# PSUM banks by name, key loads in pairs, softmax sums inverted for four blocks at once, first output products inside the attention

## The chip, the core and the metric

The kernel runs on one core of one Trainium2 chip. Its engines each work through an instruction list in order: TensorE (PE, and PEld for its weight loads) multiplies matrices into PSUM, VectorE (DVE) does element-wise work and reductions, ScalarE (ACT) copies and exponentials, GpSimd (POOL) further element-wise work, and SyncE (SP) issues the DMA transfers. The metric is the time of one execution on the device in microseconds (us).

## The reference

One layer of a block with two branches: top-k sparse attention (a) and multi-scale pooling (b), joined by gates. Sequence 4096, model width 1024, 8 heads of 64 on 2 groups of keys, 128 queries to a block. Cut to what matters:

```
proj = rms_norm(x, norm_g) @ w_in             # q k v, index qi ki wi, z_a, u_b, z_b, gates
# attention, for each block of 128 queries:
iscore = sum_h relu(qi_h . ki) * wi_h          # over allowed (chunk-causal) keys
_, idx = lax.top_k(iscore, 256)
a = (softmax(q . k[idx] / 8) @ v[idx]) * silu(z_a)
b = multiscale_pool(u_b, pool_w, pool_scale) * silu(z_b)
y = sigmoid(g_a) * (a @ w_branch_a) + sigmoid(g_b) * (b @ w_branch_b)
out = x + y @ w_out
```

## The kernel before

All products run in three float32r passes over a high and a low part (high x high, high x low, low x high). The "split" of a tile makes these parts: ScalarE copies the high part, VectorE subtracts it (lines 235 and 237 for weights, 1440 and 1441 for activations).

The program has five stages. `phase1` (to 442 us) normalizes x, projects q, k, v and the index parts, and stores rows in DRAM (`hlD`, `rowD`, `hD`). `phase_index` (442 to 2086) computes the index scores and their top-k threshold, and between them the dense products of gates and pooling (lines 1043 to 1045). `phase_exact` (to 2099) is a branch that is skipped here. `phase_attention` (2099 to 3564) runs 64 units (b, g): query block b = 0 to 31, key group g = 0 and 1, each with b + 1 tiles of 128 keys. `phase_out` (3564 to 4316) runs 16 column blocks c of 256 tokens: 16 products of 12 matmuls (8 row blocks m of y, for branch a and branch b, lines 1475 to 1477, tile `pa`), the gates (1503, 1508), and the output product (tile `po`).

From `phase_index` on a `Plan` sets the order. Steps are added with an engine, a cost and a key; `Plan.run` plays them through with these costs and writes each engine's instructions in the resulting order, the smallest key first among those that can start. A ring of buffers (`pl.ring`, `pl.new`) holds a step back until a buffer is free; `pl.have` puts a tile in a given place of a ring. On the chip each engine then keeps that order, and waits where a semaphore isn't set yet.

In a unit of the attention TensorE computes logits a first time for the row maxima (tile `ps`, line 1267), which VectorE reduces (1273) and combines (`mf`, 1279). SP stores the maxima and reads them back into `qm` (1281, 1282). TensorE then computes the transposed logits (`st`, 1306 and 1307), VectorE adds the bias (1310), ScalarE takes the exponential (1313), TensorE multiplies with v (`pv`, 1322) and sums over keys (1358, with GpSimd's running sums `acc`, 1337). ScalarE copies the sums (`sm`, 1362); SP stores them (1369) and reads them back, spread over partitions (`rl`, 1371); VectorE inverts them (1372) and SP stores the inverses (`invD`, 1373). `phase_out` reads `invD` (tile `r`, 1461) and multiplies. Loads of keys (`k4`) and of v are issued block by block, and TensorE turns the keys (335). Near the end of the attention the weights of the branches are loaded through the ring `raw` in pieces of 256 columns (229) and split (`wb`, then `wa`).

At the border of `phase1` and `phase_index` the first dense product takes a PSUM bank that the last projection (tile `ma`, read by line 417) had used. The last block's index key `k31` is loaded from `hlD` and turned on TensorE with key -50 (line 706). `guess` starts with a small product (line 629) on a tile that lines 601 and 602 write.

## Time and profile before

| | us |
|---|---|
| median of three runs | 4315.23 |
| lowest and highest | 4313.32 and 4319.19 |
| the profiled execution | 4317.85 |
| its span, first to last instruction | 4316.1 |
| TensorE busy in the span | 4154.3 (96%) |
| VectorE busy | 3223.0 (75%) |
| mean granted clock of TensorE | 0.982 |

The span is what the profile divides up; 1.75 us of the profiled execution lie around it. A wait is read as "instruction <- what ended its wait: total, times, longest". In an operation's name the tile that is written stands ahead of the arrow. A granted clock of 1.00 is 2.4 GHz, and 0.5 is 1.2 GHz; a window's number is the mean over it.

### The profile page before, as it was taken

How to read it: one execution, taken by the hardware profiler on the slowest of the kernel's cores; microseconds unless marked ns; L12 is line 12 of the kernel's file. 1: busy time of each engine (PE TensorE's matmuls, PEld its weight loads, DVE VectorE, ACT ScalarE, POOL GpSimd, SP SyncE). 2: the span in 40 equal slices, each digit the busy share in tenths (PEclk: the TensorE clock that was granted, in tenths of full speed). 3: DMA queues.
4: the chain of work that ended last, by engine and by line, in shares of the span. 5: the costliest groups of instructions: out<-in, count | busy, mean ns of one | idle time of the engine just before them, and what ended most of it. 6: DMA issues, size and time to landing. Idle time of an engine off the chain costs nothing. (4 is left out here: it accounts for less than half of the span.)

```text
span 4316.1 us, 77051 instructions
## 1 busy us (share of the span) xinstructions
PE 4154.3 (96%) x27746; PEld 3497.2 (81%) x27747; DVE 3223.0 (75%) x7858; ACT 2347.8 (54%) x3993; POOL 1904.1 (44%) x1717
## 2 busy tenths in 40 slices
PE   8999899999999999999789999999999997999999
PEld 7989899999998999999556666666666656999998
DVE  5555688888889788787568889999999994434342
ACT  5444687777777877887355555555555552111110
POOL 3454222323224332010057788888999981111110
PEclk9999999999999999999799999999999998999999
DMA  6666544545444446666532212222211116444442
GB/s 224 246 242 235 191 163 168 181 175 184 160 172 163 162 167 213 208 230 212 145 65 63 59 44 45 49 49 52 45 37 38 24 31 198 149 133 152 137 142 81
DMA packets 461117, 586.36 MB, mean 136 GB/s; under 512 B 165886, under 2 KB 358970, under 8 KB 456507
## 3 DMA queue, kind: packets, MB, share of 16 engines
q1 hardware_dynamic: 460730, 581.40, 41.9%
q8 instruction: 219, 3.59, 0.4%
q14 instruction: 168, 1.37, 0.1%
HBM read 388.54 MB, written 175.54 MB: 131 GB/s over the span
## 5 line engine op out<-in xcount | busy, mean ns | idle before, releaser
L1043 PE MATMUL pd<-h,wgh 128*128 128x256 f32 x3584 | 1019.6, 284 | 9.6 <-ACT row L417 8.2
L1044 PE MATMUL pd<-h,wgh 128*128 128x256 f32 x3584 | 1012.7, 283 | 0.0
L1045 PE MATMUL pd<-h,wgl 128*128 128x256 f32 x3584 | 1012.0, 282 | 0.0
L1337 POOL TENSOR_TENSOR acc<-acc,tt 128x1024 f32<-128x1024 f32 x388 | 925.5, 2385 | 114.0 <-ACT tt L1313 92.5
L1313 ACT ACTIVATE tt<-tt 128x512 f32<-128x512 f32 x1056 | 652.7, 631 | 583.2 <-DVE tt L1310 580.4
L1310 DVE TENSOR_TENSOR tt<-st,bT 128x512 f32<-128x512 f32 x1056 | 694.0, 685 | 65.8 <-PE st L1307 60.0
L1043 PEld LDWEIGHTS pd<-h,wgh 128*128 128x128 f32 x3584 | 681.2, 190 | 28.1 <-ACT row L417 8.5
L761 DVE SCALAR_TENSOR_TENSOR ring<-rl,wi,ring 128x1024 f32<-128x1024 f32 (+7 forms) x624 | 690.6, 1149 | 11.3 <-ACT rl L759 8.5
L1044 PEld LDWEIGHTS pd<-h,wgh 128*128 128x128 f32 x3584 | 682.0, 190 | 14.7
L1273 DVE CUSTOM_DVE_ANT_0 jk<-ps,bias 128x1024 bf16<-128x1024 f32 (+7 forms) x640 | 656.1, 1029 | 34.5 <-PE ps L1267 33.6
L1045 PEld LDWEIGHTS pd<-h,wgl 128*128 128x128 f32 x3584 | 681.9, 190 | 0.0
L759 ACT ACTIVATE rl<-ps 128x1024 f32<-128x1024 f32 (+7 forms) x624 | 539.4, 890 | 133.3 <-PE ps L756 61.4
L1322 PE MATMUL pv<-tt,vv 128*64 128x256 f32 x4224 | 527.9, 391 | 0.0
L846 ACT ACTIVATE sg<-ring,tk 128x2048 fp8e4<-128x2048 f32 (+7 forms) x322 | 485.4, 1509 | 37.3 <-DVE tk L833 21.2
L1306 PE MATMUL st<-qa,kk 128*128 128x512 f32 x1056 | 456.2, 432 | 15.9 <-DVE tt L1310 14.6
L1322 PEld LDWEIGHTS pv<-tt,vv 128*64 128x64 f32 x4224 | 280.8, 138 | 212.1 <-issue 76.8
L1307 PE MATMUL st<-qm,kl 65*128 65x512 f32 x1056 | 422.0, 400 | 3.2 <-DMA qm<-maxD 3.2
L1508 POOL TENSOR_TENSOR ga<-ga,gb 128x256 f32<-128x256 f32 x128 | 102.8, 810 | 638.8 <-DVE gb L1503 386.6
L1267 PE MATMUL ps<-kk,qa 128*128 128x512 f32 (+3 forms) x1152 | 363.0, 392 | 17.8 <-DVE mx L1273 17.7
L756 PE MATMUL ps<-kis,qT 128*128 128x512 f32 (+3 forms) x1136 | 335.1, 382 | 13.3 <-ACT rl L759 13.2
L1440 ACT ACTIVATE yh<-ga 128x256 fp32r<-128x256 f32 x128 | 53.5, 418 | 521.1 <-PE po L1476 314.4
L1306 PEld LDWEIGHTS st<-qa,kk 128*128 128x128 f32 x1056 | 200.4, 190 | 162.3 <-DVE tt L1310 59.3
(322 smaller groups left out, 7816.3 us busy)
## 6 DMA issues: line engine op xcount, KB each, us to landing
h<-hD SPq DMA_DIRECT2D x192, 1024.0 KB
hlD<-rhl SPq DMA_DIRECT2D x32, 1280.0 KB
gD<-sgm SPq DMA_DIRECT2D x256, 128.0 KB
x<-x SPq DMA_DIRECT2D x32, 512.0 KB
wraw<-w_in SPq DMA_DIRECT2D x32, 512.0 KB
hD<-hh SPq DMA_DIRECT2D x32, 512.0 KB
hD<-hl SPq DMA_DIRECT2D x32, 512.0 KB
q<-hlD SPq DMA_DIRECT2D x32, 512.0 KB
```

What stands on the lines that cost most here:

```text
L759: r = pl.add("act", 0.05 + n * 0.834e-3, k_, lambda ps=ps, rl=rl, n=n: act.activation(rl.t[:, :n], ps.t[:, :n], AF.Relu), [m], use=[ps, rl])
L761: prev[o] = pl.add("dve", 0.1 + n * 1.04e-3, k_, lambda rl=rl, o=o, n=n, h=h: v.scalar_tensor_tensor(acc[:, o:o + n], rl.t[:, :n], self.wi ...
L846: mine.append(pl.add("act", 0.28 + m * 0.834e-3, key, lambda sg=sg, o=o, m=m, e=e, j=j, b=b: act.activation(sg.t[:, o:o + m], where[b][:, ...
L1043: pe.matmul(out, wh.t[:, k], r1, start=(k == 0), stop=False)
L1044: pe.matmul(out, wh.t[:, k], r2, start=False, stop=False)
L1045: pe.matmul(out, wl.t[:, k], r1, start=False, stop=(k == KT - 1))
L1273: v.tensor_tensor_reduce(out=jk.t[:, :n], in0=ps.t[:, :n], in1=BI[b][0].t[:, o:o + n], scale=1.0, scalar=-3e38, op0=OP.add, op1=OP.max, ac ...
L1306: pe.matmul(s.t, kk[:, g, o], qa.t[:, hs], start=True, stop=False)
L1310: ad = pl.add("dve", 0.602, i, lambda s=s, tt=tt, r=r, kt=kt: v.tensor_tensor(tt.t[:, r], s.t, bc(bt.t[:, kt:kt + 1], [P, 4, P]), op=OP.ad ...
L1313: E[kt] = pl.add("act", 0.52, i, lambda tt=tt, r=r: act.activation(tt.t[:, r], tt.t[:, r], AF.Exp), [ad], use=[tt])
L1322: pe.matmul(pv.t[64 * f:64 * f + 64], vv[:, k, 64 * g:64 * g + 64], T[k // 2].t[:, k % 2, 2 * f:2 * f + 2], start=(k == 0), stop=(k == b))
L1337: gp.tensor_tensor(acc.t, first, tt.t, op=OP.add)
```

## The change

- **Index border.** Six `pl.have` lines fix which PSUM banks come first in `phase_index`. The turn of `k31` gets key 12 in place of -50.
- **Keys.** `k4` and v are loaded for two blocks by one DMA each; the ring has two buffers of twice the size.
- **Sums.** A unit only stores its sums. After the eighth unit of four blocks, `inverse` adds one load of 128x32, one reciprocal and one store, with keys 12 and 18 after the unit's end. The last four blocks are inverted in `phase_out` (key 100), and r loads of those blocks wait for it.
- **Tail.** Weights are loaded in pieces of 512 columns, ring of two. Split b and the gates of column block 0 are loaded inside the attention, and its first four products of branch b are written there. `wa`'s second half is loaded in `phase_out`; `wo` is waited for by column half. The order of products is b 4, b 5, a 0, a 1, b 6, b 7, a 2 to a 7 in block 0, and b ahead of a elsewhere.

The core of the diff:

```diff
-K4 = 4
+K4 = 2
 DIR = 4
-CL = 2
-WOK = 30.0
+WOK = 45.0
 WOD = 0.0
 PVN = 4
+IVL = 12.0
...
-            cs = slice(c, c + self.w)
-
-            def load(raw=raw, cs=cs):
+            cs = slice(o, o + w)
+
+            def load(raw=raw, o=c * CH + o):
                 for p0, r0, n, src in rows:
-                    self.queue.dma_start(raw.t[p0:p0 + n], src[r0:r0 + n, cs])
+                    self.queue.dma_start(raw.t[p0:p0 + n], src[r0:r0 + n, o:o + w])
             s = pl.add("dma", 1.4, key - 20, load, after, use=[raw])
...
+
+        for name, i in (("ps", 0), ("pd", 0), ("pd", 1), ("pd", 2), ("pt", 0), ("ps", 1)):
+            pl.have(name, i)
...
-        s3 = pl.add("pe", 0.06, -50, lambda: self.turn(pk.t[:, 0], k31), [sk], use=[pk])
+        s3 = pl.add("pe", 0.06, 12, lambda: self.turn(pk.t[:, 0], k31), [sk], use=[pk])
...
         def keys(b, base):
 
-            rows = slice(b * P, (b + 1) * P)
-            k4, pt = new("k4"), new("st")
+            k4 = new("k4")
 
             def load():
-                sp_dma(k4.t.rearrange("p g c -> p (g c)").bitcast(F32), self.hlD[rows, H_K:H_QI])
-                sp_dma(vv[:, b], self.rowD[rows, R_V - R_QI:])
+                two = slice(b * P, (b + 2) * P)
+                sp_dma(k4.t.rearrange("p t g c -> p t (g c)").bitcast(F32),
+                       self.hlD[two, H_K:H_QI].rearrange("(t p) c -> p t c", p=P))
+                sp_dma(vv[:, b:b + 2], self.rowD[two, R_V - R_QI:].rearrange("(t p) c -> p t c", p=P))
...
             s3 = pl.add("dma", 0.2, end + FD, store_sums, [s2], use=[sm])
-            s4 = pl.add("dma", 0.2, end + FD, lambda: sp_dma(rl.t, flat(self.sumD)), [s3], [rl])
-            s5 = pl.add("dve", 0.12, end + FD + FE, lambda: v.reciprocal(rl.t, rl.t), [s4], use=[rl])
-            pl.add("dma", 0.2, end + FD + FE, lambda: sp_dma(flat(self.invD), rl.t), [s5], use=[rl])
+            summed.setdefault(b // 4, []).append(s3)
+            if len(summed[b // 4]) == 8 and u < len(units) - 1:
+                self.inverse(pl, b // 4, end + IVL, summed[b // 4])
...
-                first += 1
+                first += 2
...
-        pl.ring("raw", 3, lambda i: self.wp.tile([P, CH // 2], F32, name=f"raw{i}"))
-        src = a["w_branch_a"][0]
-        self.wa, self.wb = (Weights(self, pl, n, 4, nc.sync, CH // 2) for n in ("wa", "wb"))
+        w2 = 2 * P
+        pl.ring("raw", 2, lambda i: self.wp.tile([P, CH], F32, name=f"raw{i}"))
+        for name, bufs, dt in (("o", 1, F32), ("bh", 2, F32R), ("bl", 2, F32R), ("gb", 2, F32)):
+            pl.ring(name, bufs, lambda i, name=name, dt=dt: self.wp.tile([P, 2, w2], dt, name=f"{name}{i}"))
+        self.wa, self.wb = (Weights(self, n, 4, nc.sync) for n in ("wa", "wb"))
...
+        for c in range(2):
+            for k in range(4):
+                self.wb.put(pl, c, k, E0 - 40 + c * 10, [(0, k * P, P, a["w_branch_b"][0])], lambda: self.wp, CH, [s])
...
+                s1 = pl.add("pe", 1.32, E0 + PRE + m, mm, [x[2] for x in xs] + self.wb.steps[0], use=[ps])
...
         for k in range(4):
-            self.wb.put(k, at[-1] - 40, [(0, k * P, P, a["w_branch_b"][0])], lambda: self.wp, [s])
-        for k in range(4):
-            self.wa.put(k, at[-1] - 20, [(0, k * 64, 64, src), (64, 256 + k * 64, 64, src)], lambda: self.wp, [s])
+            self.wa.put(pl, 0, k, E0 - 15, self.rows_a[k], lambda: self.wp, CH, [s])
...
+    def inverse(self, pl, n, key, after):
+
+        nc = self.nc
+        rl = pl.new("rl")
+
+        def flat(d):
+            return bass.AP(tensor=d.tensor, offset=d[4 * n].offset, ap=[[32, P], [1, 32]])
+        s = pl.add("dma", 0.2, key, lambda: nc.sync.dma_start(rl.t, flat(self.sumD)), after, [rl])
+        s = pl.add("dve", 0.12, key + 6, lambda: nc.vector.reciprocal(rl.t, rl.t), [s], use=[rl])
+        return pl.add("dma", 0.2, key + 6, lambda: nc.sync.dma_start(flat(self.invD), rl.t), [s], use=[rl])
...
+        pl.ring("rl", 1, lambda i: sp.tile([P, 32], F32, name=f"rl{i}"))
+        inv = self.inverse(pl, NB // 4 - 1, 100.0, [])
+        pl.ring("raw", 4, lambda i: (self.wp if i < 2 else sp).tile([P, CH], F32, name=f"raw{i}"))
...
-                s2 = pl.add("dma", 1.0, key - 15, spread, use=[r])
+                s2 = pl.add("dma", 1.0, key - 15, spread, [inv] if 2 * c >= NB - 4 else [], use=[r])
...
-        for k in range(KT):
-            wo.put(k, WOK + k * WOD, [(0, k * P, P, a["w_out"][0])], lambda: sp)
+        for k in range(4):
+            self.wa.put(pl, 1, k, 12.0, self.rows_a[k], lambda: sp, CH)
+        for c in range(2):
+            for k in range(KT):
+                wo.put(pl, c, k, WOK + 4 * c, [(0, k * P, P, a["w_out"][0])], lambda: sp, CH)
...
-            lag = CL if c == 0 else 0
-            for m, b in sorted(((m, b) for m in range(8) for b in "ba"), key=lambda x: (x[0] + lag * (x[1] == "a"), x)):
+            if c == 0:
+                out = {(m, "b"): (first["gb"][m // 2], None) for m in range(4)}
+            order = sorted(((m, b) for m in range(8) for b in "ba"), key=lambda x: x[0] + (x[1] == "a") * (2 if c == 1 else 0.5))
+            if c == 0:
+                order = [(4, "b"), (5, "b"), (0, "a"), (1, "a"), (6, "b"), (7, "b")] + [(m, "a") for m in range(2, 8)]
+            for m, b in order:
...
-                             lambda k, i, fs=fs: wo.parts[i][:, k, fs], wo.steps + [y[2] for y in Y], key,
+                             lambda k, i, fs=fs: wo.get(i, k, fs), wo.steps[f] + [y[2] for y in Y], key,
```

**Index border, TensorE.** Before: the dense product (`pd`) with line 335's turn of the key, then line 629; `qi` are the index queries.

```order
L1045 MATMUL pd_5325<-h_4959,wgl_4972 128x256
L335 MATMUL pt_5344<-identr,k_5260 128x128
L1043 MATMUL pd_5325<-h_4959,wgh_4971 128x256
L1044 MATMUL pd_5325<-h_4961,wgh_4971 128x256
L1045 MATMUL pd_5325<-h_4959,wgl_4972 128x256
L1043 MATMUL pd_5325<-h_4959,wgh_4971 128x256
L1044 MATMUL pd_5325<-h_4961,wgh_4971 128x256
L1045 MATMUL pd_5325<-h_4959,wgl_4972 128x256
L629 MATMUL pd_5353<-ring 128x1
L335 MATMUL pt_5355<-identr,qi_5314 128x128 x4
```

The turn stands inside the second set of dense matmuls.

After, the same place (line numbers are those of the changed file: 1052 to 1054 the dense product, 635 the small product, 341 the turns):

```order
L1052 MATMUL pd_5331<-h_4959,wgh_4971 128x256
L1053 MATMUL pd_5331<-h_4961,wgh_4971 128x256
L1054 MATMUL pd_5331<-h_4959,wgl_4972 128x256
L635 MATMUL pd_5356<-ring 128x1
L341 MATMUL pt_5358<-identr,qi_5320 128x128 x4
L1052 MATMUL pd_5331<-h_4959,wgh_4971 128x256
```

The key's turn is gone from here; it stands later, and six more dense matmuls stand ahead of the small product.

**Early attention, VectorE.** Before, `tt` is the bias addition, `jk` and `mx` the maxima, `rl` the sums to invert:

```order
L1372 RECIPROCAL rl_29208<-rl_29208 128x4
L1273 ISA jk_29238,mx_29171<-ps_29222,bias_28856 128x768
L1273 ISA mx_29171 128x1
L1310 TENSOR_TENSOR tt_29249<-st_29231,bT_28986 128x512
L1310 TENSOR_TENSOR tt_29249<-st_29241,bT_28986 128x512
L1273 ISA jk_29269,mx_29270<-ps_29244,bias_29039 128x896
L1273 ISA mx_29270 128x1
L1279 TENSOR_REDUCE mf_29274<-mx_29171 128x4
L1310 TENSOR_TENSOR tt_29276<-st_29251,bT_28986 128x512
L1273 ISA jk_29282,mx_29270<-ps_29255,bias_29039 128x896
L1273 ISA mx_29270 128x1
L1372 RECIPROCAL rl_29267<-rl_29267 128x4
```

One reciprocal stands there for each unit, between maxima and additions.

After, around the first reciprocal of a group:

```order
L1286 ISA jk_29306,mx_29247<-ps_29292,bias_29025 128x896
L1286 ISA mx_29247 128x1
L1323 TENSOR_TENSOR tt_29299<-st_29301,bT_29121 128x512
L1323 TENSOR_TENSOR tt_29333<-st_29316,bT_29121 128x512
L1286 ISA jk_29337,mx_29338<-ps_29321,bias_29025 128x896
L1286 ISA mx_29338 128x1
L1292 TENSOR_REDUCE mf_29353<-mx_29247 128x4
L1464 RECIPROCAL rl_29244<-rl_29244 128x32
L1323 TENSOR_TENSOR tt_29333<-st_29348,bT_29121 128x512
L1286 ISA jk_29365,mx_29338<-ps_29355,bias_29025 128x896
L1286 ISA mx_29338 128x1
L1323 TENSOR_TENSOR tt_29374<-st_29361,bT_29121 128x512
```

The reciprocal after each unit is gone; one of 128x32 stands there for eight units.

**Output border, SP.** Before, from the last sums on: `raw` are weights on their way, `o`, `z` and `r` the parts of the branches' inputs:

```order
L1371 DMA rl_42525<-sumD 128x4
L229 DMA raw_42527<-w_branch_a 64x256 x2
L229 DMA raw_42532<-w_branch_a 64x256 x2
L229 DMA raw_42538<-w_branch_a 64x256 x2
L1373 DMA invD<-rl_42525 128x4
L1452 DMA o_42559<-bD 128x2x256
L1452 DMA o_42561<-bD 128x2x256
L1455 DMA o_42563<-oD 128x2x256
L1456 DMA z_42565<-gD 128x2x256
L1461 DMA r_42571<-invD 64x2x128 x4
```

The loads of `o`, `z` and `r` stand behind the weights and the last sums' way out and back.

After, from the last weight piece of the attention on:

```order
L234 DMA raw_42129<-w_branch_a 64x512 x2
L1388 DMA oD<-ov_42210 64x2x128 x2
L1379 DMA sumD<-sm_42227 1x256 x2
L1514 DMA z_42286<-gD 128x2x256
L1519 DMA r_42301<-invD 64x2x128 x4
L1513 DMA o_42306<-oD 128x2x256
L1514 DMA z_42308<-gD 128x2x256
L1519 DMA r_42311<-invD 64x2x128 x4
L1562 DMA ga_42319<-gD 128x2x256
L234 DMA raw_42323<-w_branch_a 64x512 x2
```

The last sums' load and their inverses' store no longer stand here, and the loads of branch b stand earlier.

**Output border, TensorE.** After, the end of the attention: `ps_42168` and `ps_42214` are the first two of the four products of branch b:

```order
L1444 MATMUL ps_42168<-bl_41968,wb_41847 128x256
L1444 MATMUL ps_42168<-bh_41953,wb_41848 128x256
L1335 MATMUL pv_41902<-tt_42134,vv 64x256 x4
L1335 MATMUL pv_41902<-tt_42160,vv 64x256 x4
L1371 MATMUL st_42191<-acc_41914,ones 64x256 x2
L1371 MATMUL st_42191<-tt_42090,ones 64x256 x4
L1371 MATMUL st_42191<-tt_42119,ones 64x256 x4
L1371 MATMUL st_42191<-tt_42134,ones 64x256 x4
L1371 MATMUL st_42191<-tt_42160,ones 64x256 x4
L1444 MATMUL ps_42214<-bh_41882,wb_41847 128x256
```

Before, the last `pv` and the sums of line 1358 follow each other, and the first product of branch b stands behind them as `pa`. Now one product stands ahead of the last `pv`, and three follow the sums.

## Rows read from the trace of the kernel before

**Rows 1.** Windows: us; busy us (count) of PE, PEld, DVE, ACT, POOL; clock, DMA.

```profile
2147.00:2530.00 383.00, 353.43 (x2023) 225.99 (x2021) 308.70 (x631) 197.66 (x368) 261.91 (x130) 0.96 0.29 61
2530.00:3500.00 970.00, 969.66 (x5672) 642.36 (x5671) 918.94 (x1706) 524.60 (x913) 869.43 (x387) 1.00 0.18 40
3564.00:3625.00 61.00, 36.27 (x221) 32.92 (x218) 31.62 (x62) 20.05 (x40) 8.13 (x8) 0.76 0.63 187
```

**Rows 2.** Waits of VectorE, 2090 to 2560: total us, times, longest.

```profile
DVE rl L1372 <- DMA rl<-sumD: 51.8, 24, 5.4
```

**Rows 3.** Waits of TensorE, 2147 to 2530.

```profile
PE ps L1267 <- DVE mx L1273: 17.1, 11, 4.5
PE st L1306 <- DVE tt L1310: 8.8, 8, 3.7
```

**Rows 4.** Chain of waits, shares by line: 2147 to 2530, then 2530 to 3500.

```profile
by line: PE pv L1322 18.7%; PE ps L1267 10.2%; PE st L1306 10.1%; PE st L1307 8.1%; DMA rl<-sumD 7.1%; issue 4.7%; DVE tt L1310 4.2%; DVE jk L1273 3.8%; DMA sumD<-sm 3.2%; PE st L1358 1.8%; PE st L335 1.7%; DMA maxD<-mf 1.5%; ACT tt L1313 0
...
by line: PE pv L1322 36.6%; PE st L1306 22.0%; PE ps L1267 19.3%; PE st L1307 18.1%; PE st L1358 1.6%; PE st L335 1.5%; DMA rl<-sumD 0.4%; DMA sumD<-sm 0.1%; SPq L1378 0.1%; DVE tt L1310 0.1%; ACT qa L1232 0.1%; ACT qm L1233 0.0%; issue 0.0
```

**Rows 5.** Groups by line, the bias addition: 2147 to 2530, then 3000 to 3500.

```profile
L1310 DVE TENSOR_TENSOR tt<-st,bT 128x512 f32<-128x512 f32 x245 | 161.9, 684 | 17.9 <-PE st L1307 16.5 <-issue 0.6 <-PE ps L1267 0.2
...
L1310 DVE TENSOR_TENSOR tt<-st,bT 128x512 f32<-128x512 f32 x395 | 259.4, 685 | 16.5 <-PE st L1307 13.9 <-POOL acc L1337 0.6
```

**Rows 6.** Waits of TensorE, 440 to 470.

```profile
PE pd L1043 <- ACT row L417: 8.2, 1, 8.2
PE pt L335 <- DMA k<-hlD: 6.1, 1, 6.1
```

**Rows 7.** Timeline of ScalarE and VectorE, 460 to 465.5: start, us, instruction, wait ahead.

```profile
462.62 0.31 ACT L572 ACTIVATE wm0h<-sgm 128x128 fp32r<-128x128 f32 x1 [5.96 <-DMA sgm<-pool_w]
...
464.57 0.17 DVE L602 MEMSET ring<- 128x128 f32 x1
```

**Rows 8.** Waits of TensorE, 3564 to 3640.

```profile
PE pa L1475 <- ACT bh L1440: 16.6, 1, 16.6
PE po L1475 <- ACT yh L1440: 5.5, 1, 5.5
PE pa L1475 <- ACT ah L1440: 2.0, 1, 2.0
```

**Rows 9.** Timeline of SyncE's DMA issues, 3562 to 3580.

```profile
3566.14 0.67 SPq L1369 DMA_DIRECT2D sumD<-sm  x2
...
3575.05 0.59 SPq L1373 DMA_DIRECT2D invD<-rl  x1
```

**Rows 10.** Pieces of the chain, 3555 to 3625: start, us, what.

```profile
3559.38 2.28 DMA raw<-w_branch_a
...
3570.69 1.77 DMA rl<-sumD
...
3577.18 6.59 DMA z<-gD
...
3585.06 3.33 DMA r<-invD
...
3614.16 3.92 DMA raw<-w_out
```

**Rows 11.** Windows after 3581, columns as in rows 1.

```profile
3581.00:3588.00 7.00, 6.44 (x30) 5.65 (x30) 3.97 (x6) 1.26 (x2) 0.00 (x0) 0.66 0.76 192
...
3597.00:3616.00 19.00, 19.00 (x148) 18.24 (x146) 12.80 (x26) 8.70 (x17) 5.54 (x5) 1.00 0.61 186
```

**Rows 12.** Groups by line from 3516 and 3564, timelines of DVE and POOL from 3524.

```profile
L237 DVE TENSOR_TENSOR wb<-raw,wb 128x256 fp32r<-128x256 f32 x16 | 21.4, 1337 | 0.0
...
L237 DVE TENSOR_TENSOR wo<-raw,wo 128x512 fp32r<-128x512 f32 x16 | 10.8, 688 | 3.3 <-ACT wo L235 3.0
...
3525.57 2.00 DVE L237 TENSOR_TENSOR wb<-raw,wb 128x256 fp32r<-128x256 f32 x1
...
3524.84 15.04 POOL L1337 TENSOR_TENSOR acc<-acc,tt 128x1024 f32<-128x1024 f32 x6
```

More of the change, by code (lines that the diff above doesn't have):

```diff
@@ L51 @@
 QB = 3
-WQ = 0
+PRE = 4
 OV = 2
@@ new lines, in phase_attention @@
+        self.wa, self.wb = (Weights(self, n, 4, nc.sync) for n in ("wa", "wb"))
+        self.rows_a = [[(0, k * 64, 64, a["w_branch_a"][0]), (64, 256 + k * 64, 64, a["w_branch_a"][0])] for k in range(4)]
+        s = pl.add("dma", 0.1, at[-1] - 60, room, done)
+        E0 = at[-1]
+        self.first = {"gb": []}
+        for c in range(2):
+            for k in range(4):
+                self.wb.put(pl, c, k, E0 - 40 + c * 10, [(0, k * P, P, a["w_branch_b"][0])], lambda: self.wp, CH, [s])
+        xs = []
@@ new lines, in phase_attention @@
+        for i in range(2):
+            o, h, l = new("o"), new("bh"), new("bl")
+            s1 = pl.add("dma", 1.0, E0 - 45, lambda o=o, i=i: sp_dma(
+                o.t, self.bD[2 * i:2 * i + 2, :, 0:w2].rearrange("k p c -> p k c")), [s], use=[o])
+            s1 = pl.add("act", 0.52, E0 - 25, lambda o=o, h=h: act.activation(h.t, o.t, AF.Copy), [s1], use=[o, h])
+            s1 = pl.add("dve", 0.61, E0 - 25, lambda o=o, h=h, l=l: v.tensor_tensor(
+                l.t, o.t, h.t.bitcast(F32), op=OP.subtract), [s1], use=[o, h, l])
+            xs.append((h, l, s1))
@@ new lines, in phase_attention, with mm @@
+        for i in range(2):
+            g = new("gb")
+            s0 = pl.add("dma", 1.0, E0 - 45, lambda g=g, i=i: sp_dma(
+                g.t, self.gD[8 + 2 * i:10 + 2 * i, :, 0:w2].rearrange("k p c -> p k c")), [s], use=[g])
+            for m in (2 * i, 2 * i + 1):
+                ps = new("ps")
+                def mm(ps=ps, m=m):
+                    ms = slice(m * P, (m + 1) * P)
+                    for k in range(4):
+                        for x, y in ((0, 0), (0, 1), (1, 0)):
+                            pe.matmul(ps.t[:, :w2], self.wb.get(x, k, ms), xs[k // 2][y].t[:, k % 2],
+                                      start=(k == x == y == 0), stop=(k == 3 and x == 1))
+                s1 = pl.add("pe", 1.32, E0 + PRE + m, mm, [x[2] for x in xs] + self.wb.steps[0], use=[ps])
+                pl.add("dve", 0.34, E0 + PRE + m, lambda g=g, ps=ps, m=m: v.tensor_tensor(
+                    g.t[:, m % 2], ps.t[:, :w2], g.t[:, m % 2], op=OP.mult), [s0, s1], use=[g, ps])
+            self.first["gb"].append(g)
@@ L1429, in phase_out @@
                       "al": (AB, two, F32R), "bh": (AB, two, F32R), "bl": (AB, two, F32R), "ga": (GB, two, F32),
-                      "gb": (GB, two, F32), "yh": (YB, one, F32R), "yl": (YB, one, F32R)}),
+                      "gb": (3, two, F32), "yh": (YB, one, F32R), "yl": (YB, one, F32R)}),
                 (pp, {"pa": (4, [P, CH], F32), "po": (2, [P, CH], F32)})):
             for name, (bufs, shape, dt) in rings.items():
-                pl.ring(name, bufs, lambda i, name=name, pool=pool, shape=shape, dt=dt: pool.tile(
-                    shape, dt, name=f"{name}{i}"))
+                pl.ring(name, bufs, lambda i, name=name, pool=pool, shape=shape, dt=dt: (
+                    self.wp if i < kept.get(name, 0) else pool).tile(shape, dt, name=f"{name}{i}"))
+        first = {n: [pl.have(n, i, x.t) for i, x in enumerate(self.first[n])] for n in ("bh", "bl", "gb")}
         def split(key, name, src, after, n):
@@ L1487, in phase_out @@
             cs = slice(c * w2, (c + 1) * w2)
-            X = {b: [load(c, k, c * T - LDC, b) for k in (0, 2)] for b in "ba"}
+            X = {b: [load(c, k, c * T - LDC, b) if c or b == "a" else (first["bh"][k // 2], first["bl"][k // 2], None)
+                     for k in (0, 2)] for b in "ba"}
             Y, out, G = [], {}, {}
-            lag = CL if c == 0 else 0
-            for m, b in sorted(((m, b) for m in range(8) for b in "ba"), key=lambda x: (x[0] + lag * (x[1] == "a"), x)):
+            if c == 0:
[4 more added lines that the diff above has]
+            for m, b in order:
                 key = c * T + m * T / 8
@@ L1498, in phase_out @@
                 g, s0 = G[b]
-                x, pa, w = X[b], new("pa"), wa if b == "a" else wb
-                s1 = product(4, lambda pa=pa: pa.t[:, :w2], lambda k, i, w=w, ms=ms: w[i][:, k, ms],
-                             lambda k, i, x=x: x[k // 2][i].t[:, k % 2], [y[2] for y in x] + [s1], key,
+                x, pa, w = X[b], new("pa"), self.wa if b == "a" else self.wb
+                s1 = product(4, lambda pa=pa: pa.t[:, :w2], lambda k, i, w=w, ms=ms: w.get(i, k, ms),
+                             lambda k, i, x=x: x[k // 2][i].t[:, k % 2], [y[2] for y in x] + [s1] + (
+                                 self.wa.steps[1][-4:] if c == 0 and b == "a" and m >= 4 else []), key,
                              [pa] + [h for y in x for h in y[:2]], w2)
```

64 lines of the change are left out of this document (35 added, 29 removed).

## The prediction

> **What bounds the kernel now.** I read the busy time of each engine by stage first, then what TensorE and VectorE wait for, then the chain of waits. In the late attention (2530 to 3500 us) TensorE is busy in all but 0.34 of 970 us at full clock, with VectorE at 918.94: nothing there waits, and only work taken off TensorE itself could shorten it [rows 1]. In the early attention (2147 to 2530) it is busy in 353.43 of 383 us, and VectorE, with 308.70, is not full either: the two engines stop in turns. The largest wait of VectorE in the early part is the reciprocal of line 1372, which waits for the load of the sums just stored: 51.8 us in 24 waits [rows 2]. VectorE works in its written order, so the maxima and the bias additions behind that reciprocal stop too, and TensorE then waits for exactly these: 17.1 us for maxima and 8.8 us for additions [rows 3]. The chain of waits in that stretch gives 7.1% to that load and 3.2% to the store ahead of it, that is 27.2 + 12.3 = 39.5 of 383 us; in the late attention the two have 0.4% and 0.1%, 4.9 of 970 us [rows 4].
>
> Two other idle places are borders. At 442 us TensorE waits 8.2 us for a PSUM bank that ScalarE's copy of line 417 still reads, then 6.1 us for a key load [rows 6]. After 3564 us it waits 16.6 us for the first split of branch b, 2.0 for branch a and 5.5 for the first y [rows 8], and works at part of its clock between the waits: 0.66 granted at 3581 to 3588 against 1.00 after 3597 [rows 11]. The stretch 3564 to 3625 holds only 36.27 us of TensorE work in 61 us [rows 1].
>
> **Sums inverted late, for four blocks at once.** This removes 64 loads, reciprocals and stores and adds 8 of each. In the new order VectorE's reciprocal of a group stands about two units of maxima behind the position at which SP issues its load in the first groups, and about one unit or less in the last. The load itself was 1.77 us in the chain at the output border [rows 10]; a unit of the early attention lasts several times that (245 score tiles in 383 us are 1.56 us a tile, and a unit of block b has b + 1 of them) [rows 5]. So I cost the eight new waits at 0, covered by the additions and maxima between. If that cover is gone at all eight places, they cost 8 x 1.77 = 14 us. On SP the loads wait in line for the last of eight stores, as each load did before; behind them stand stores of maxima and loads of queries, which now meet 8 such stops in place of 64.
>
> What of the 51.8 us comes back? Not less, in principle, than TensorE's own idle time behind VectorE, 17.1 + 8.8 = 25.9 us [rows 3], and not more than the 39.5 us of the chain unless the engines fall into step better than now. A check by rate: 395 tiles took 500 us in the late part, 1.27 us each; at that rate 245 tiles are 310 us, 73 less than the stretch took [rows 5]. Early units are short, so what each unit pays once (sums, turns of the queries) weighs more on a tile, and part of the 73 stays. I take 33 us, the middle of 25.9 and 39.5. For the range: down to 15, should VectorE, with 308.70 of 383 us busy, be late next for its own work and half of TensorE's idle time stay; up to 45. The late attention gives 0 to 4.9; I take 3. Next late is what rows 3 name without the reciprocal: TensorE's scores waiting for a free bank behind VectorE's maxima.
>
> **Order of PSUM banks, turn of the last key.** No work is removed. The first bank of the dense product is now one that is free at 442, and the key's turn stands behind 42 dense products in place of 36. TensorE can then do these 42 from 442 on. But the next thing in its order, the product of line 629, needs the memset of line 602 at 464.57, which stands on VectorE behind ScalarE's splits of the pool weights at 462.62, which wait 5.96 us for their load [rows 7]. None of these moves on its queue. TensorE stood at line 629 at about 465 and will stand there again, with its idle time in one piece. I take 0, between -14.3 (both waits gone, 8.2 + 6.1) and +2 (a clock that rises again later).
>
> **Keys in pairs.** 64 load issues become 32, with the same bytes. A turn that waits for its pair waits for the larger load; the first query's load, which ends the wait at the start of the attention, stands behind the same number of issues. I take 0, from -1 to +1.
>
> **First products in the attention's tail.** Removed from the border: the last sums' round trip on SP (load at 3570.69 [rows 10], store at 3575.05, then the first loads of the output stage [rows 9]), 16 narrow weight loads for branch b become 8 wide ones, half of branch a's move behind the border, and 4 of the 16 products of the first column block are done early. One product is 12 matmuls; 148 matmuls took 19.00 us [rows 11], so one is about 1.5 us and four are 6. The walk: TensorE ends the sums at about 3564 as now and goes on at once with three of these products and two more of branch b, to about 3571.5. Branch a needs z and r, whose issues stand behind the store of the last sums (now at 3566.14 [rows 9]). The z load took 6.59 us and the r load 3.33 [rows 10]; with the weights of a no longer ahead, I put the last of them at 3574 to 3576 and the first product of a at 3574 to 3577: 2 to 6 us idle. The next product of b needs a PSUM buffer freed by VectorE behind the splits of branch a's second half: 3 to 5 us idle. The first output product needs the halved w_out loads, the last of which landed in 3.92 us [rows 10]: 0 to 5 us idle, and 1.5 for the first y. Together 6.5 to 17.5 us idle where 16.6 + 2.0 + 5.5 = 24.1 were [rows 8]. The stretches at half clock cost now: 0.66 over 7 us and the like twice more, about 8 us; with two or three gaps again I keep 5 to 8. With one product (1.5 us) already done before the sums, the gain is 24.1 - 17.5 + 0 + 1.5 = 8 to 24.1 - 6.5 + 3 + 1.5 = 22. I take 12, nearer the lower end, since each gap above is one of SP's order, which is issued at about 0.6 us an entry.
>
> Rows 11 show that TensorE came back from 16.6 us of idleness at a clock of 0.66 and was at 1.00 from 3597 on. The Trainium skill, "TensorE: Matmul & The Clock Gate", section "What's actually happening", states that idle TensorE drops to 1.2 GHz and only sustained work lifts it to 2.4. The trace agrees. By this rule several short gaps could keep the five early b products at the lower level: 5 x 1.5 = 7.5 us lost, and the border would gain 4 or 5 in place of 12. I leave it at the bottom of the term's range, 2.
>
> In the attention's tail itself 16 splits of 256 columns become 14 of 512 (8 of wb, 2 of b, 4 of wa). Alone a split of 512 takes 688 ns. Beside GpSimd's running sums the 16 took 1337 ns each, 21.4 us in all; the one of 2.00 us began at 3525.57 and ended at 3527.57, just after GpSimd's second 2.51 us step from 3524.84 began (six in 15.04 us) [rows 12]. So a split waits for GpSimd's instruction to end and then runs: the wait is per instruction, not per column. 14 x (1.34 + 0.3) = 23 us, against 21.4: within 2 us, taken as 0.
>
> **Sum.** 33 + 3 + 0 + 0 + 12 = 48 us. The profiled execution took 4317.85 us, so its like would take 4269.9; the median of the three runs, 4315.23, is 2.6 lower, and I forecast 4315.23 - 48 = 4267 us.
>
> **Rivals.**
> First, the reciprocal's waits only hid what VectorE and TensorE need anyway. For it: VectorE is at 81% in the stretch, 94.7% in the late part [rows 1]. The early term is 15, the late one 0, and the time 4315 - 15 - 12 = 4288. Against it: the chain gives the load 7.1%.
> Second, all of the 51.8 us comes back: 4315 - 52 - 5 - 12 = 4246. Against it: TensorE has only 29.6 us of idle time in that stretch.
> Third, the index border gives its 14.3 us as well: 4253. It needs line 602 to be early, and rows 7 speak against that. That the new order there gains nothing is what I forecast.
> Fourth, the split beside GpSimd loses time by columns, not by instructions: 14 x 2.67 = 37 in place of 21.4 us, and VectorE is full in that stretch, so 16 us on the end: 4283. The Trainium skill, "GPSIMD Engine Reference", section "Specifications", says that GpSimd shares its SBUF interfaces with VectorE and contends with instructions of two SBUF inputs; a contention shared element by element would give this time. The ends in rows 12 speak for whole instructions.
> Fifth, slower: the wide weight loads of the tail have a ring of two and their splits stand between the bias additions on VectorE and the exponentials on ScalarE. Were no load to overlap another's split, a round would be two issues (1.2), landing (2.28 to 3.92 [rows 10]), ScalarE's half (0.6), VectorE's (0.7 to 2): up to 7.7 us, and 12 rounds 92 us where the stretch of rows 12 has 41 now: +51, which with the attention's 36 us and the border's 12 gone makes 4315 - 36 + 51 = 4330. It turns slower than before from 12 rounds of 6.4 us on (77 against 41 + 36), that is if landing takes nearly its longest at every round. Two to five additions stand between a split and the next but one, and landing was 2.28 us, so the overlap should hold.
>
> **Chances.** Forecast 0.52, first rival 0.20, second 0.10, third 0.06, fourth 0.07, fifth 0.05. The range must leave out no more than 2 in 10: from 4238 (second rival with 20 at the output border) to 4298 (first rival with 2 there). About 0.2%, 8.6 us, is what a measurement of this kernel can tell from no change: faster than 4306.6 has 0.90, within 0.06, slower 0.04.
>
> **What would show it.** Right: in the early attention no wait of VectorE for the load of sums worth naming, TensorE's busy share there above 0.97, and the late attention as before within 5 us. At 442 us one wait of TensorE for line 602 or its product up to 465. At the output border TensorE's waits of 10 to 17 us in three pieces. Wrong: a new wait of the 128x32 reciprocal, a wait of ScalarE's or VectorE's splits for weights inside the attention's tail, or the early stretch still long with VectorE full.

## The result and the profile after

| | before | after |
|---|---|---|
| median of four runs, us | 4314.4 | 4263.1 |
| lowest and highest | 4313.32, 4319.19 | 4260.26, 4264.02 |
| ratio, 95% interval | | 0.9878 [0.9861, 0.9895] |
| profiled execution, us | 4317.85 | 4264.02 |
| its span, us | 4316.1 | 4262.3 |
| TensorE busy, us | 4154.3 | 4137.7 |

The kernel became 51 us faster; 48 were forecast, and the median of 4267 that was forecast lies 4 us above the one measured. To see where the time went I compare where the same matmuls start in the two traces, so that each stretch holds the same work. A score tile is one tile `st` of 128 keys for a unit; the 192nd matmul of the output product (`po`) is the last of the second column block.

| stretch, by starts of matmuls | before, us | after, us | gained | forecast |
|---|---|---|---|---|
| start to the first transposed logits of the attention (`st`) | 2123.7 | 2127.2 | -3.5 | 0 |
| to the 300th score tile (early attention) | 466.6 | 426.8 | 39.8 | 33 |
| to the 1000th (late attention) | 894.9 | 896.0 | -1.1 | 3 |
| to the last sum of the attention (its tail) | 78.7 | 81.6 | -2.9 | 0 |
| to the 192nd matmul of the output product (border) | 142.8 | 121.3 | 21.5 | 12 |
| to the last matmul | 605.3 | 605.2 | 0.1 | 0 |

The windows of the early attention, from the first score tile to the 300th, in the columns of [rows 1]: the stretch, busy us (and counts) of PE, PEld, DVE, ACT and POOL, then the clock. Of before:

```profile
2123.70:2590.30 466.60, 432.77 (x2441) 276.30 (x2440) 377.15 (x785) 240.15 (x445) 312.63 (x154) 0.95 0.29 61
```

and of after:

```profile
2127.20:2554.00 426.80, 417.81 (x2437) 273.11 (x2437) 375.52 (x755) 238.84 (x445) 313.26 (x154) 0.97 0.30 66
```

TensorE was idle for 33.8 us of it and is now for 9.0. That is 24.8 us. The other 15.0 us are busy time, 432.77 against 417.81, for the same work, at a mean clock of 0.95 against 0.97. The windows of the stretch in which the granted clock was 0.50, added up, six of before and four of after (their length, then the busy time of each engine):

```profile
sum 44.90, PE 38.25 PEld 22.05 DVE 27.70 ACT 15.86 POOL 13.68; mean PE 6.37 PEld 3.68 DVE 4.62 ACT 2.64 POOL 2.28
...
sum 21.20, PE 18.31 PEld 10.47 DVE 7.05 ACT 8.36 POOL 2.53; mean PE 4.58 PEld 2.62 DVE 1.76 ACT 2.09 POOL 0.63
```

So 20 us less of TensorE's work ran at the lower clock. At the output border of the changed kernel matmuls of one product start 0.12 us apart at 1.00 and 0.21 at 0.50; by that, an estimate, the clock makes about 9 of the 15.0 us. The other 6 weren't traced. VectorE's waits, 2090 to 2560, are now

```profile
DVE tt L1323 <- PE st L1320: 23.2, 36, 3.0
DVE jk L1286 <- PE ps L1280: 20.0, 31, 3.8
DVE jk L1286 <- POOL bT L1256: 8.4, 1, 8.4
```

with no wait for the load of the sums among them (51.8 us in [rows 2]); the engine waits for TensorE instead, which is now the bound. In the chain of waits of 2147 to 2530 the load of the sums is no longer among the large shares (7.1% in [rows 4]); the store ahead of it still has 1.2% (3.2% before):

```profile
by line: PE pv L1335 34.4%; PE st L1319 20.4%; PE ps L1280 18.6%; PE st L1320 16.4%; PE st L1371 3.8%; PE st L341 3.1%; DMA sumD<-sm 1.2%; SPq L1259 0.7%; SPq L1388 0.3%; DVE jk L1286 0.3%; issue 0.2%; ACT sm L1375 0.2%; SPq L1379 0.2%; SPq
```

The eight reciprocals of groups take twice the 0.17 us that one of a unit took (count, then shortest, median and longest in ns, first and last start):

```profile
L1464 DVE RECIPROCAL rl<-rl x8: 343/346/353, 2198.7 to 3636.3; 128x32 f32<-128x32 f32 x8
```

At the index border TensorE's waits, 440 to 475, are

```profile
PE pd L635 <- DVE ring L608: 18.3, 1, 18.3
PE pt L341 <- DMA qi<-hlD: 0.6, 1, 0.6
```

where [rows 6] had 8.2 and 6.1. TensorE did its 42 dense matmuls at once (42 stand ahead of the small product in both kernels, before with the key's turn among them) and then stood 18.3 us for the memset (line 608 of the changed file, 602 before), which came at 466.26 behind ScalarE's split at 464.31 (464.57 and 462.62 in [rows 7]):

```profile
464.31 0.31 ACT L578 ACTIVATE wm0h<-sgm 128x128 fp32r<-128x128 f32 x1 [5.97 <-DMA sgm<-pool_w]
...
466.26 0.17 DVE L608 MEMSET ring<- 128x128 f32 x1
```

At the output border TensorE's waits from 3531 to 3610 are these, against the 24.1 us of [rows 8]:

```profile
PE pa L1533 <- ACT ah L1498: 5.4, 3, 2.6
PE pa L1534 <- DVE al L1499: 1.0, 3, 0.3
PE pa L1533 <- DVE gb L1570: 0.6, 1, 0.6
PE po L1533 <- DVE raw L1589: 0.3, 1, 0.3
```

On SP the z and r loads stand directly behind the store of the last sums: the first z load is issued 1.5 us behind the last sum (which starts at 3531.6), where it was 13.2 us (3577.18 [rows 10], the last sum at 3564.0):

```profile
3532.45 0.55 SPq L1379 DMA_DIRECT2D sumD<-sm  x2
3533.10 0.39 SPq L1514 DMA_DIRECT2D z<-gD  x1
3533.53 2.56 SPq L1519 DMA_DIRECT2D r<-invD  x4
```

The clock is at 1.00 from the last sum to the first waits. After these it was at its lower level for 3.3 us, with TensorE busy all the time (0.66 in the mean of 7 us in [rows 11]):

```profile
3531.00:3536.30 5.30, 5.30 (x46) 4.77 (x43) 0.85 (x2) 0.39 (x1) 0.00 (x0) 1.00 0.25 77
...
3541.40:3551.00 9.60, 6.66 (x41) 6.46 (x41) 5.43 (x10) 3.78 (x7) 1.96 (x2) 0.82 0.62 196
...
3544.90:3548.20 3.30, 3.30 (x16) 3.30 (x17) 1.71 (x3) 1.56 (x4) 1.11 (x1) 0.50 0.67 207
```

### The profile page after: what moved, and what is told of

It is laid out like the page before. It is cut to its first block, busy times and chain, and to the rows that moved or that the text cites. A ratio compares the mean times of both kernels' runs of the same rounds, so it can differ in the third digit from the quotient of the medians.

```text
span 4262.3 us, 76690 instructions
## 1 busy us (share of the span) xinstructions
PE 4137.7 (97%) x27746; PEld 3492.4 (82%) x27747; DVE 3217.1 (75%) x7786; ACT 2344.9 (55%) x3977; POOL 1903.4 (45%) x1717
## 4 chain that ended last, share of the span: by engine, by line
PE 47%; DVE 1%; DMA 1%; POOL 1%; issue 0%; ACT 0%; SPq 0%; DVEq 0%; POOLq 0%; ACTq 0%
PE pv L1335 11%; PE st L1319 7%; PE ps L1280 6%; PE st L1320 6%; PE po L1533 3%; PE po L1534 3%; PE po L1535 3%; PE pa L1534 3%; PE pa L1535 3%; PE pa L1533 3%; PE st L1371 1%; PE st L341 1%; POOL acc L1350 0%; DVE tt L1323 0%; DMA maxD<-mf 0%
## 5 line engine op out<-in xcount | busy, mean ns | idle before, releaser
L770 DVE SCALAR_TENSOR_TENSOR ring<-rl,wi,ring 128x1024 f32<-128x1024 f32 (+7 forms) x624 | 692.1, 1153 | 12.9 <-ACT rl L768 10.3
```

Of the source, the lines that this page charges most:

```text
L770: prev[o] = pl.add("dve", 0.1 + n * 1.04e-3, k_, lambda rl=rl, o=o, n=n, h=h: v.scalar_tensor_tensor(acc[:, o:o + n], rl.t[:, :n], self.wi ...
```

## The experiments

Ten kernels were run, each against the kernel before on the same chip. Two columns give the stretches of the table above that the experiment was made for.

| run | median, us | before beside it | ratio [95%] | to 300th tile, us | last sum to 192nd output, us |
|---|---|---|---|---|---|
| before | 4314.4 | | 1 | 466.6 | 142.8 |
| changed | 4263.1 | 4314.4 | 0.9878 [0.9861, 0.9895] | 426.8 | 121.3 |
| s_undone | 4304.65 | 4312.88 | 0.9981 [0.9971, 0.999] | 461.5 | 125.5 |
| s_late_single | 4278.93 | 4312.88 | 0.9915 [0.9898, 0.9931] | 441.0 | 125.7 |
| s_batch_early | 4265.6 | 4312.88 | 0.9887 [0.987, 0.9903] | 428.2 | 121.7 |
| s_alone | 4277.58 | 4312.88 | 0.9916 [0.99, 0.9933] | 429.9 | 140.6 |
| t_undone | 4280.0 | 4315.49 | 0.9919 [0.9903, 0.9936] | 429.1 | 141.6 |
| t_256 | 4264.25 | 4315.49 | 0.9885 [0.9868, 0.9901] | 428.8 | 121.3 |
| i_undone | 4263.55 | 4315.49 | 0.988 [0.9864, 0.9897] | 427.0 | 121.5 |
| i_late | 4262.17 | 4315.49 | 0.9877 [0.986, 0.9893] | 427.0 | 121.9 |
| p_out | 4262.28 | 4314.36 | 0.9882 [0.9865, 0.9898] | 427.9 | 123.3 |
| k_undone | 4262.87 | 4314.36 | 0.9883 [0.9867, 0.99] | 425.9 | 121.4 |

### The sums: the wait, its place, and the number of round trips

**s_undone** takes the sums alone back to one inversion per unit:

```diff
-            summed.setdefault(b // 4, []).append(s3)
-            if len(summed[b // 4]) == 8 and u < len(units) - 1:
-                self.inverse(pl, b // 4, end + IVL, summed[b // 4])
+            s4 = pl.add("dma", 0.2, end + FD, lambda: sp_dma(rl.t, flat(self.sumD)), [s3], [rl])
+            s5 = pl.add("dve", 0.12, end + FD + FE, lambda: v.reciprocal(rl.t, rl.t), [s4], use=[rl])
+            pl.add("dma", 0.2, end + FD + FE, lambda: sp_dma(flat(self.invD), rl.t), [s5], use=[rl])
```

> The changed kernel with the sums inverted unit by unit at the old places again; all else as changed. Theory W (what was gained in the early attention is VectorE's wait for the load of the sums, set by where the reciprocal stands): the milestone of the 300th score tile, which came 36 us earlier in the changed kernel, falls back by 35 to 40 us, VectorE waits some 50 us for the load again, time 4298 to 4304. Rival K (part of the gain in the early attention comes from the keys in pairs or the freer SP queue): VectorE's waits return but the time rises by no more than 25, 4280 to 4288.

Measured: 4304.65, and the early attention is back at 461.5 us. VectorE's wait, 2090 to 2560:

```profile
DVE rl L1385 <- DMA rl<-sumD: 46.8, 21, 3.8
```

The time is 8.2 us under the kernel before beside it, where the changed kernel is 51.3 under its own: by the medians 43 of the 51 us go with the sums. The profile shows less: the profiled execution was the fastest of ten (4298.76, the slowest 4311.12), and its early attention is 34.7 us longer than in the changed kernel's profile. The rest of the 43 wasn't traced. Theory W holds but for its edges: the time is 0.65 us over the upper one, and 34.7 us came where 35 to 40 were expected. Rival K falls.

**s_alone** is the kernel before with only the new sums (the diff of the change, the lines of `inverse` and those that call it).

> The kernel before with only the sums changed. Theory W: the early attention gains 36 to 40 us alone, the border to the output stage 0 to 5 (the last round trip on SP is gone), time 4270 to 4279. Rival K (the other parts are needed for it): 4285 to 4300.

Measured: 4277.58, 35 us under the kernel before beside it. The early attention takes 429.9 us, as in the changed kernel but for 3.1 us, so the sums need no help of the other parts there, and theory W holds. The border stays at 140.6 us, 2.2 less: with the old output stage the last round trip on SP was worth only that. With the new one it is worth about 4 (125.5 in s_undone and 125.7 in s_late_single against 121.3).

**s_late_single** keeps one round trip per unit, at the new late place:

```diff
-            if len(summed[b // 4]) == 8 and u < len(units) - 1:
-                self.inverse(pl, b // 4, end + IVL, summed[b // 4])
+            s4 = pl.add("dma", 0.2, end + IVL, lambda: sp_dma(rl.t, flat(self.sumD)), [s3], [rl])
+            s5 = pl.add("dve", 0.12, end + IVL + 6, lambda: v.reciprocal(rl.t, rl.t), [s4], use=[rl])
+            pl.add("dma", 0.2, end + IVL + 6, lambda: sp_dma(flat(self.invD), rl.t), [s5], use=[rl])
```

> The changed kernel with one load, reciprocal and store per unit as before, but at the late places (12 and 18 us of the plan behind the unit's end) and with four buffers. Theory W (the place of the reciprocal decides, not the number): no wait of VectorE for the load over 2 us in all, 56 more reciprocals of 0.18 us are 10 us of VectorE work under TensorE's, time 4262 to 4270. Rival N (the number of round trips on SP and VectorE decides): at least half of the 40 us is lost, 4283 to 4303.

Measured: 4278.93, between the two theories' ranges, so neither holds alone. The late place gives 25.6 of the 39.8 us of the early attention (466.6 to 441.0). What remains is four waits, 2090 to 2560:

```profile
DVE rl L1385 <- DMA rl<-sumD: 11.1, 4, 5.7
```

In this order up to three reciprocals follow each other on VectorE and up to three stores of inverses on SP. The waits add up to 11.1 us, and the early attention is 14.2 longer than in the changed kernel.

**s_batch_early** is the opposite: one inversion for four blocks, at the old early place.

```diff
-IVL = 12.0
+IVL = 4.0
-        s = pl.add("dve", 0.12, key + 6, lambda: nc.vector.reciprocal(rl.t, rl.t), [s], use=[rl])
+        s = pl.add("dve", 0.12, key + FE, lambda: nc.vector.reciprocal(rl.t, rl.t), [s], use=[rl])
```

> The changed kernel with the sums inverted for four blocks at once, but at the old early places (4 and 6 us of the plan behind the unit's end). Theory W: of the 24 waits of 51.8 us before, the three groups that end in the early attention wait, 2 to 5 us each, 6 to 15 us of VectorE in all, of which most reaches the end: 4268 to 4278. Rival N (the number decides): no loss over 3 us, 4260 to 4266.

Measured: 4265.6, its ratio within the interval of the changed kernel's, the early attention at 428.2 us, and VectorE waits, 2090 to 2560, only

```profile
DVE rl L1464 <- DMA rl<-sumD: 1.9, 2, 1.6
```

Rival N holds: the time lies in its 4260 to 4266. Theory W had expected 6 to 15 us of waits and at least 4268, and was too high. Of the two levers, measured by the early attention, fewer round trips (64 to 8) does nearly all of it alone, 38.4 of 39.8 us; the late place alone does about two thirds. Together they are hardly more than the first.

### The output border

**t_undone** has the old tail and output stage (weights in pieces of 256, no input, gates or products of branch b in the attention) with all else changed.

```diff
-                self.wb.put(pl, c, k, E0 - 40 + c * 10, [(0, k * P, P, a["w_branch_b"][0])], lambda: self.wp, CH, [s])
...
+            self.wb.put(k, at[-1] - 40, [(0, k * P, P, a["w_branch_b"][0])], lambda: self.wp, [s])
```

> The kernel before with sums, bank order and paired keys as changed, and the old tail and output stage: only the tail is undone. Theory T (the 21.5 us between the last sum and the 192nd output matmul come from the early loads, splits and products of branch b): that stretch is within 3 us of the kernel before, the attention's last sum 2 to 6 us earlier than in the changed kernel (fewer splits of 512 columns beside GpSimd), time 4276 to 4281. Rival R (the last sums' round trip on SP is what was gained): 4263 to 4268.

Measured: 4280.0, and 141.6 us from the last sum to the 192nd output matmul. TensorE waits there, 3527 to 3620, as it did before:

```profile
PE pa L1494 <- ACT bh L1459: 12.3, 2, 9.7
PE po L1494 <- ACT yh L1459: 5.6, 1, 5.6
PE pa L1494 <- ACT ah L1459: 4.3, 3, 2.5
```

The tail of the attention, from the 1000th tile to the last sum, is 77.8 us, 3.8 shorter than in the changed kernel. So the new tail and output stage gain 20.3 us at the border and give 3.8 back ahead of it, and by the medians 16.9 us are left of it. Theory T holds, rival R falls.

**p_out** moves the four products back to the output stage and leaves branch b's loads and splits in the attention:

```diff
-                s1 = pl.add("pe", 1.32, E0 + PRE + m, mm, [x[2] for x in xs] + self.wb.steps[0], use=[ps])
...
-                order = [(4, "b"), (5, "b"), (0, "a"), (1, "a"), (6, "b"), (7, "b")] + [(m, "a") for m in range(2, 8)]
+                order = [(m, "b") for m in range(6)] + [(0, "a"), (1, "a"), (6, "b"), (7, "b")] + [(m, "a") for m in range(2, 8)]
```

> The changed kernel with the loads and splits of branch b's input still inside the attention, but its first four products and their gates' loads back in the output stage (order b 0 to b 5, a 0, a 1, b 6 and on). Theory P (doing the products early is part of the gain): 1.5 us for the product that stood ahead of the last sums and 2 to 5 us for gates that land behind z and r, so that the fifth product waits for a PSUM buffer: 4266 to 4270. Rival Q (the early loads alone are the gain, TensorE goes from the sums into the same products either way): 4262 to 4265.

Measured: 4262.28; rival Q holds in time. As theory P said, TensorE does wait for a PSUM buffer, 8.6 us from 3520 to 3600:

```profile
PE pa L1516 <- DVE gb L1551: 8.6, 2, 6.5
```

but these 8.6 us take the place of the 7.3 us that the changed kernel waits at the border (6.4 of them for branch a), and the border is 2.0 us longer, the tail 0.6 shorter. The early products themselves brought nothing that can be measured. With b's input and weights split before the last sum the 12.3 us of waiting for `bh` in t_undone are gone; what of the rest of the gain is due to that, and what to the new order of products and to the weights waited for by halves, no run separates; the width of the weight pieces isn't it, since t_256 has the border at 121.3 too.

**t_256** loads the tail's weights in pieces of 256 columns:

```diff
-                self.wb.put(pl, c, k, E0 - 40 + c * 10, [(0, k * P, P, a["w_branch_b"][0])], lambda: self.wp, CH, [s])
+                self.wb.put(pl, c, k, E0 - 40 + c * 10, [(0, k * P, P, a["w_branch_b"][0])], lambda: self.wp, CH // 2, [s])
```

> The changed kernel with the weights of the attention's tail in pieces of 256 columns (24 splits of 256 and 2 of 512 in place of 14 of 512), ring of four. Theory I (a split waits for the end of one GpSimd instruction, whatever its columns): 24 x 1.3 + 2 x 1.9 = 35 us of VectorE in place of 14 x 1.9 = 27, the attention's last sum 4 to 9 us later, time 4267 to 4272. Rival C (the loss goes by columns): the same VectorE time, 4262 to 4265.

Measured: 4264.25, in rival C's range. But the splits show theory I's side. In the changed kernel and in this one (groups by line, from 3470 and 3468 on; count, busy us, mean ns):

```profile
L1350 POOL TENSOR_TENSOR acc<-acc,tt 128x1024 f32<-128x1024 f32 x17 | 43.0, 2528 | 3.2 <-ACT tt L1326 2.0
...
L243 DVE TENSOR_TENSOR wb<-raw,wb 128x512 fp32r<-128x512 f32 x8 | 15.1, 1887 | 0.6 <-ACT wb L240 0.6
```

```profile
L1350 POOL TENSOR_TENSOR acc<-acc,tt 128x1024 f32<-128x1024 f32 x17 | 40.9, 2409 | 6.2 <-ACT tt L1326 5.1
...
L243 DVE TENSOR_TENSOR wb<-raw,wb 128x256 fp32r<-128x256 f32 x16 | 22.0, 1382 | 0.1
```

A split of twice the columns takes 1887 ns against 1382, which is 505 ns more and not twice, so 16 narrow ones cost VectorE 6.9 us more than 8 wide ones. That didn't reach the end: the tail is 81.2 us in the one and 81.6 in the other. VectorE's time for the splits does not set the tail, contrary to both theories' premise. What makes the changed tail 3 to 4 us longer than the old one is open. TensorE is busy for 75.46 us in it and idle for 6.2, against 73.19 and 5.6 before; one product of about 1.4 us stands ahead of the last sums. But p_out, without that product, has 73.07 busy and 7.9 idle, so the product isn't the one cause.

### The index border and the keys

**i_undone** takes the bank order and the key of the turn back.

```diff
-        for name, i in (("ps", 0), ("pd", 0), ("pd", 1), ("pd", 2), ("pt", 0), ("ps", 1)):
-            pl.have(name, i)
-        s3 = pl.add("pe", 0.06, 12, lambda: self.turn(pk.t[:, 0], k31), [sk], use=[pk])
+        s3 = pl.add("pe", 0.06, -50, lambda: self.turn(pk.t[:, 0], k31), [sk], use=[pk])
```

> The changed kernel with the old bank order and the old key of the last index key's turn. Theory L (TensorE stands for the small product's operand either way): TensorE waits 8.2 + 6.1 us in two pieces again, the small product starts within 1.5 us of where it did, time 4259 to 4264; should the 2 to 4 us by which the index stage ended later be an effect of the new order, they come back. Rival B (the new order hid a part of these waits): the small product or the end of the index stage is 4 us later or more, 4267 to 4277.

Measured: 4263.55, as the changed kernel; TensorE's waits are the old ones again, 440 to 475:

```profile
PE pd L1049 <- ACT row L423: 8.4, 1, 8.4
PE pt L341 <- DMA k<-hlD: 6.2, 1, 6.2
```

and the small product starts at 465.8 us (466.5 in the changed kernel, 465.2 before). 14.6 us of waits in two pieces or 18.3 in one: the time is the same. Theory L holds. The 3.5 us by which the attention began later in the changed kernel's profile are not settled as an effect: in the profiles of the eight kernels with the new index order the first matmul of `phase_exact` (it adds up the flag that lets the branch be skipped) starts between 2098.2 and 2104.0 us, in those of the three with the old order at 2099.0 to 2099.7.

**i_late** moves the small product and the first turn of the index queries behind 36 more dense matmuls.

```diff
-        s = pl.add("pe", 0.1, key, lambda: nc.tensor.matmul(pc.t[:, 0:1], ones, ks, start=True, stop=True), [s], [pc])
+        s = pl.add("pe", 0.1, 8, lambda: nc.tensor.matmul(pc.t[:, 0:1], ones, ks, start=True, stop=True), [s], [pc])
-                s = pl.add("pe", 0.24, key, turn, [ld], use=[q, pt, t])
+                s = pl.add("pe", 0.24, 8 if b == NB - 1 else key, turn, [ld], use=[q, pt, t])
```

> The changed kernel with the small product of the index border and the first turn of the index queries moved behind 36 more dense matmuls. Theory L: these 36 x 0.12 = 4.3 us are done inside the 18.3 us wait, and since TensorE is the bound of the index stage the end comes 3 to 4.3 us earlier: 4258 to 4261. Rival V (the stage is held by the chain of the small product, VectorE and ScalarE): nothing gained or up to 4 us lost, 4262 to 4267.

Measured: 4262.17, 0.9 us under the changed kernel and inside its interval: no gain that can be told from none. TensorE did 30 of the 36 matmuls at once and then waited for a PSUM buffer, 440 to 475:

```profile
PE pd L1052 <- ACT u L957: 13.6, 1, 13.6
```

The wait shrank from 18.3 to 13.6 us as planned, the small product came 1.5 us later (468.0), and the time didn't move by what the wait lost. That first matmul of `phase_exact`, at 2099.1, is 3.6 us earlier than in the changed kernel's profile, but within what the same order showed from run to run, so whether the 4.3 us were won and lost in the spread stays open.

**k_undone** loads keys and v block by block again (`K4 = 4`, the old `keys`, `first += 1`).

> The changed kernel with keys and v loaded block by block again. Theory Z (the pairs cost and give nothing): the first score tile and the 300th stand within 1.5 us of the changed kernel's, measured from the end of the index stage, 4261 to 4265. Rival Y (the pairs delay or help the first blocks): 3 us or more either way at the 50th score tile.

Measured: 4262.87; the first score tile stands 24.7 us behind the end of the index stage (24.6 in the changed kernel and 24.7 before), the 50th 115.9 (117.2 in the changed kernel), and the early attention takes 425.9 us. The pairs cost and give nothing: theory Z.

## Why the prediction was right

The time fell into the range, near its middle, and for the main reason given. That it came within 4 us is in part luck: the sums and the output border were forecast 6.8 and 9.5 us too small, and the late attention, the tail and the start, 4.1, 2.9 and 3.5 too large, took most of that back.

- **Sums, early attention: right mechanism, 33 forecast, 39.8 measured.** The step that was mis-sized is the choice of a middle between 25.9 us (TensorE's idle time behind VectorE, [rows 3]) and 39.5 us (the store and load in the chain, [rows 4]). On the same work, from the 9th score tile to the 254th, 383.6 us before (2146.5 to 2530.1) and 344.9 after (2149.1 to 2494.0), 38.7 were gained. So the chain had it to 1 us. Of the 38.7, 25.7 are idle time, just the lower price, and 12.9 are busy time, which that price left out: matmuls were longer where TensorE stopped often, about 9 of the 15.0 us of the whole stretch by the lower clock. The first rival, that the waits hid VectorE's own need, falls: VectorE went from 81% to 88% busy over the same tiles (377.15 of 466.60, 375.52 of 426.80) and does not bind. The cost of 0 for the eight new waits held; no such wait shows.
- **Late attention: 3 forecast, -1.1 measured,** and 0.8 in s_alone. The 4.9 us of the chain there did not come back. [rows 1] had it: TensorE was idle for 0.34 of these 970 us, so no more than that could come from a wait; to take 3 from the chain was the step that failed.
- **Index border: 0 forecast, confirmed** with the very step that was named, the wait for line 602, and by i_undone; i_late couldn't tell its gain from none. What was left out is that the end of that stage varies by 6 us from profile to profile, which is more than the 3.5 by which the attention began later.
- **Keys: 0, confirmed.**
- **Output border: 12 forecast, 21.5 measured, at the top of the walk's 8 to 22.** The step that was mis-sized is "nearer the lower end". The waits were 7.3 us in eight pieces, at the short end of the walk's 6.5 to 17.5 and below the 10 to 17 in three pieces that were named as the sign: the first product of a started 8.2 us after the last sum (10 to 13 forecast; VectorE could use z 3.8 us after its issue, where the load took 6.59 [rows 10]); the wait for a PSUM buffer was 0.6 us (3 to 5 forecast) and that for the first output product 0.3 (0 to 5). p_out shows another thing that I had not asked: the early products are not what brought it; the early loads are, as far as the 12.3 us of waiting for b go.
- **Attention's tail: 0 forecast, -2.9 measured.** The fourteen wide splits were forecast at 23 us and took 21.8 (eight of `wb` 15.1, four of `wa` 4.3, two of b's input 2.4); the count left out seven narrow splits of `wa` that ran in the old tail. t_256 shows that VectorE's time for splits is not what the tail waits for. What is, stays open.
- **The two rules that were weighed.** The five products of b behind the last sum ran at a granted clock of 1.00 (3531.0 to 3541.4), so the 7.5 us that I had worked out for them at the lower level were not lost. But after waits of 0.3 to 2.6 us the clock was 0.50 from 3544.9 to 3548.2, and again from 3568.8 to 3572.1, in products of a, then of b and of the output. The Trainium skill, "TensorE: Matmul & The Clock Gate", section "What's actually happening", says that idleness lowers the clock; the trace agrees, at a smaller price: 6.6 us of work at the lower level, where the border before had 15.3. Beside GpSimd a split of `wb` took 1.2 us longer, and GpSimd's own instruction became longer too, 2528 ns beside wide splits and 2409 beside narrow ones. The Trainium skill, "GPSIMD Engine Reference", section "Specifications", says that GpSimd shares its SBUF interfaces with VectorE, with contention for VectorE instructions of two SBUF inputs; a split is one, and the traces agree. They show beside it that the loss hardly grows with the columns, so the fourth rival falls.

## What to carry to other kernels

A small DRAM round trip in the middle of an in-order engine's list cost a wait most times where units were short (24 waits, 51.8 us of VectorE) and nothing where TensorE was full; grouping eight into one removed nearly all of it, even at the old place, and moving them later alone about two thirds. When the chain of waits and an engine's idle time give two prices for the same wait, the chain's was right here where TensorE stopped often, since busy time fell with the idle time (12.9 us beside 25.7); where TensorE was full, the chain's 4.9 us brought nothing. Removing a wait at a border gives nothing while the next instruction in the same list waits for something that did not move: walk the list to the next operand that comes late, and at the other border see that the inputs are loaded early rather than the products done early.

## What the runs showed of the hardware that was not expected

- A VectorE subtraction of two SBUF tiles beside GpSimd's 2.4 us additions takes 1382 ns at 256 columns and 1887 at 512, where it takes 425 and 688 with GpSimd idle or nearly so: about 1.0 and 1.2 us more per instruction, nearly whatever its width.
- In the early attention the same matmuls took 15 us longer, in busy time, when TensorE stopped for 33.8 us in all in place of 9.0; the granted clock there was 0.95 against 0.97 on the mean of the stretch, and 38.25 against 18.31 us of the work fell into windows at 0.50.
- The same index stage reached the first matmul behind it between 2098.2 and 2104.0 us in eight traces, all of the same order of instructions there: single traces can't tell differences of 3 us.
- After four waits of 0.3 to 2.6 us between 3539 and 3545, in the changed kernel, the clock stood at 0.50 through 3.3 us of unbroken work.
